# Retention takes one finished normalized input, with three gate tiles ahead of queries and keys

## The chip, the core and the metric

The kernel runs on one core of a Trainium2 chip. The metric is the device time of one execution in microseconds; three runs of the kernel before took 1112.13, 1111.17 and 1109.13 us, median 1111.17 us. The engines are named as in the profile: PE is the matrix engine (PEld its weight loads), DVE the vector engine, ACT the scalar engine, POOL GpSimd, SP the engine that issues the loads.

## The reference

Two layers; each is a SwiGLU half step, a token mixer and a second SwiGLU half step, all on a normalized and modulated input. The mixer of layer 0 is retention, that of layer 1 a short convolution. For x of 256 tokens by 1024 features the mixer's part is:

```python
h = modulate(x, norm_g[l, 1], shift[:, 1], scale[:, 1])  # x / rms(x) * g * (1 + scale) + shift
proj = h @ w_in                                          # q, k: 4 heads x 256; v: 4 x 512; g: 2048
q = rotary(q, pos)
k = rotary(k, pos) * (dk ** -0.5)
# x1 * cos - x2 * sin, x2 * cos + x1 * sin
o = ...            # decayed causal attention per head: (q k^T * decay) v, in chunks
o = rmsnorm(o, gn_g.reshape(H, dv))
y = (jax.nn.silu(g) * o.reshape(B, S, H * dv)) @ w_out
x = x + gate[:, 1, None, :] * y
```

## The kernel before

Features lie on the 128 partitions, tokens along the free dimension; x is eight blocks of 128 x 256. Every float32 operand of a large product is split in two halves, a high one and a low one (type fp32r); a product is high x high + high x low + low x high, so three matmuls for each 128 x 128 block of weights (`product`, lines 273 to 287). Where the two halves of the moving operand lie side by side and the result has room for both, the first two are one matmul of 512 columns (line 283); otherwise they are two (lines 285 and 286), and line 287 is the third.

Weights come in tiles of 2048 columns, 16 blocks of 128, in the order of the list `jobs` (lines 199 to 218); `weights()` takes the next one, keeps four loads ahead and every now and then adds a load of conditioning weights whose reduction runs on DVE (line 119). Each tile is split in two parts of 1024: the high half by ACT (line 243), the low half by DVE or, for some, POOL (line 248). Buffers hold three split tiles (six parts).

While x gets its last residual, the next stage's input is already prepared as h = x * scale, not yet divided by the rms and without the shift (`scaled`, lines 374 to 397). Each h block has 256 token columns and two more columns that hold the shift, so each matmul streams 258 columns, and a projection leaves in column 256 what the shift contributes. r = 1/rms is applied when the result is taken out of PSUM: `normalized` (lines 302 to 308) multiplies a pair of output blocks, 2 x 258, by r; the shift's part is then added as a bias. `modulated` (lines 411 to 423) starts the first tile before r is known and hands it on as `begun`.

Retention (lines 598 to 717) runs eight query/key tiles, four value heads of two weight tiles each, eight gate tiles, eight output tiles. For each query/key tile, line 610 adds std times the shift's part, `rotate` (lines 589 to 596) makes the rotation from SBUF with six operations of 256 elements, half on POOL and half on DVE, with tables that line 603 has multiplied by r. Beside each of these tiles one block of a second input, `hv` (lines 617 to 619), is made for the values: x * scale + std * shift, in halves; it stands as the weights' side in the value products (lines 632 to 634), where r is a factor of each token, applied when the values leave PSUM (line 637); `by_token` (lines 578 to 587) turns r for that by four matmuls. Scores (lines 640 to 658), values (660 to 678) and the norm of each head (680 to 687) follow in steps, one head behind the other; the gate tiles' outputs are made one tile at a time (lines 703 to 713): Silu, product with the normalized head, split in halves on ACT and POOL.

A planner orders each engine's queue from the program's order and the operands' readiness; every engine then works through its queue in that order, and an instruction that waits holds those behind it. PSUM is four buffers of two banks. One pool of 22 slots of 128 x 512 (`slot`, line 82) holds `qk`, `hv`, `v`, `sc`, `o`, `og` and, in other stages, `act` and `conv`; a slot is free when the last reader of its tile is done.

Of the kernel before, what the change touches and what calls it, by code (L numbers as in the profile page):

```python
# [9 lines left out]
F32 = mybir.dt.float32  # L10
# [4 lines left out]
P = 128  # L15
# [15 lines left out]
LATE = 5  # L31
AHEAD = 4
# [33 lines left out]
def trunk_kernel(ctx: ExitStack, tc: tile.TileContext, a: dict, out: bass.AP):  # L66
# [135 lines left out]
    for l in range(DEPTH):  # L202
        for f in range(2):
            if f == 1:
                if l % 2 == 0:
                    jobs += [(a["ret_qk"][j], 2048) for j in range(8)]
                    jobs += [(a["ret_v"][h, i], 2048) for h in range(HEADS) for i in range(2)]
                    jobs += [(a["ret_g"][j], 2048) for j in range(8)]
# [80 lines left out]
    def projections(h, by_part=False):  # L289

        ps, w = banks(), weights()
        n = h[0].shape[-1]
# [7 lines left out]
        return ps  # L300

# [103 lines left out]
    def fill(n):  # L405

        ps = banks()[:, 1, :P]
        for _ in range(n):
            nc.tensor.matmul(out=ps, lhsT=ones, rhs=cond[:, :P], start=True, stop=True)

# [167 lines left out]
    def by_token(r):  # L578

        ps = banks()  # L580
        t = tmp.tile([P, 2], F32, name="by_token")
        for tb in range(2):
            nc.tensor.matmul(
                out=ps[:, tb, :1], lhsT=r[:1, tb * P:(tb + 1) * P], rhs=ones[:1, :1], start=True, stop=True
            )
        nc.vector.tensor_copy(out=t, in_=ps[:, :, 0])
        return [t[:, tb:tb + 1] for tb in range(2)]

    def rotate(y, cos, sin, dst):
        t = tmp.tile([P, 2, S], F32, name="rot", tag="rot")  # L590
        nc.gpsimd.tensor_tensor(out=t[:, 0, :], in0=y[:, 1, :S], in1=sin, op=ALU.mult)
        nc.vector.tensor_tensor(out=t[:, 1, :], in0=y[:, 1, :S], in1=cos, op=ALU.mult)
        nc.gpsimd.tensor_tensor(out=dst[:, :S], in0=y[:, 0, :S], in1=cos, op=ALU.mult)
        nc.gpsimd.tensor_tensor(out=dst[:, :S], in0=dst[:, :S], in1=t[:, 0, :], op=ALU.subtract)
        nc.vector.tensor_tensor(out=dst[:, S:], in0=y[:, 0, :S], in1=sin, op=ALU.mult)
        nc.vector.tensor_tensor(out=dst[:, S:], in0=dst[:, S:], in1=t[:, 1, :], op=ALU.add)

    def retention(n, h, r, std, begun):
        l, s = sublayers[n]
        cos = table[:, T_COS:T_COS + S]  # L600
        sin = table[:, T_SIN:T_SIN + S]
        for t in (cos, sin):
            nc.gpsimd.tensor_tensor(out=t, in0=t, in1=r[:, :S], op=ALU.mult)
        qk = []
        hv = []
        while len(qk) < 2 * HEADS:
            ps = projections(h) if qk else begun
            y = tmp.tile([P, 2, HALF], F32, name="sum")
            for i in range(2):
                nc.vector.scalar_tensor_tensor(  # L610
                    out=y[:, i, :S], in0=std, scalar=ps[:, i, S:S + 1], in1=ps[:, i, :S], op0=ALU.mult, op1=ALU.add
                )
            t = slot(F32, "qk")
            rotate(y, cos, sin, t)
            qk.append(t)
            k = len(qk) - 1
            xs = tmp.tile([P, S], F32, name="xs", tag="av", bufs=3)
            nc.scalar.activation(out=xs, in_=x[k], func=AF.Copy, scale=scale_t[l][s][:, k:k + 1])
            hv.append(halves(l, s, k, xs, std, in_halves(slot(F32R, "hv")))[0])
        r_tok = by_token(r)  # L620
        v = [[] for _ in range(HEADS)]

        def project_values(hd):
# [11 lines left out]
            for tb in range(2):  # L635
                t = slot(F32, "v")
                nc.scalar.activation(out=t, in_=ps[:, tb, :], func=AF.Copy, scale=r_tok[tb])
                v[hd].append(t)
# [51 lines left out]
        gated = []  # L690
        steps = [lambda hd=hd: project_values(hd) for hd in range(HEADS)]
        steps += [lambda j=j: projections(h) for j in range(8)]
        for step, run in enumerate(steps):
            got = run()
# [164 lines left out]
```

## Time and profile before

| | us |
|---|---|
| median of three runs | 1111.17 |
| the profiled execution | 1109.17 |
| its span, first to last instruction | 1107.4 |
| PE busy in the span | 1073.8 |
| DVE busy | 850.2 |
| ACT busy | 575.4 |
| POOL busy | 387.7 |

The profile is of one execution, and 1.8 us of its time lie outside its span. Busy is the time in which an engine has at least one instruction running; matmuls overlap, so the busy time of PE is not its work at its peak, and the distance between the starts of two matmuls says more than the duration of one. The retention stage begins in the profile with the first matmul of 258 columns at 206.45 us and ends with its outputs at about 428 us. Wherever the text names a line, it is a line of the kernel before.

### The profile page before, as it was taken

Reading aid. Unit: us, or ns where it says so; the run is one execution under the profiler, and the core shown is the slowest. Engines: PE = TensorE matmul, PEld = TensorE weight load, DVE = VectorE, ACT = ScalarE, POOL = GpSimd, SP = SyncE. Lnnn points to the kernel's source line nnn. Section 1 sums busy time; section 2 is a strip of 40 time slices with the busy share of each in tenths; the row PEclk is TensorE's granted clock in tenths of the full one; section 3 lists DMA queues with packets and bytes.
Section 4 is the critical chain, followed back from the end, with each engine's and each line's share of the span. In section 5 each row is a group of like instructions: output and inputs, shape, how many; then the busy total and the mean of one; then the engine's idle time right before and its main releaser. Section 6 shows DMA issues by size and latency. Waiting matters only on the chain.

```text
span 1107.4 us, 19630 instructions
## 1 busy us (share of the span) xinstructions
PE 1073.8 (97%) x7790; PEld 1019.1 (92%) x7790; DVE 850.2 (77%) x1118; ACT 575.4 (52%) x918; POOL 387.7 (35%) x345
## 2 busy tenths in 40 slices
PE   8999999997899999999999999999999989999996
PEld 7999988996779989999988999998899989999985
DVE  5999777999559888887768778776798786666354
ACT  4464454732357666455455655445565475454452
POOL 0034356344024631333355232335511532223352
PEclk9999999998999999999999999999999999999998
DMA  9977789855465777786669867667886535454441
GB/s 348 354 272 277 295 283 316 308 205 190 190 228 191 265 249 278 289 312 247 244 225 321 326 251 301 253 229 252 313 300 253 175 138 207 167 191 132 157 131 39
DMA packets 44574, 268.52 MB, mean 242 GB/s; under 512 B 4801, under 2 KB 6977, under 8 KB 19906
## 3 DMA queue, kind: packets, MB, share of 16 engines
q1 hardware_dynamic: 43138, 266.56, 66.4%
q8 instruction: 61, 1.00, 0.4%
q10 hardware_dynamic: 1344, 0.71, 0.2%
q14 instruction: 31, 0.25, 0.1%
HBM read 266.20 MB, written 1.05 MB: 241 GB/s over the span
## 4 chain that ended last, share of the span: by engine, by line
PE 58%; DVE 2%; issue 0%; ACT 0%; DVEq 0%; ACTq 0%
PE ps L287 19%; PE ps L286 14%; PE ps L285 14%; PE ps L283 10%; DVE lo L248 1%; PE ps L338 0%; DVE rsum L475 0%; DVE h L392 0%; DVE raw L781 0%; DVE r L777 0%; DVE x L478 0%; ACT hi L243 0%; DVEq L854 0%; DVE x L480 0%; ACT std L350 0%
## 5 line engine op out<-in xcount | busy, mean ns | idle before, releaser
L248 DVE TENSOR_TENSOR lo<-raw,hi 128x1024 fp32r<-128x1024 f32 (+1 forms) x300 | 363.1, 1218 | 174.8 <-ACT hi L243 144.6
L285 PE MATMUL ps<-h,hi 128*128 128x258 f32 (+1 forms) x1728 | 490.2, 284 | 3.6 <-DVE sum L610 2.5
L286 PE MATMUL ps<-h,hi 128*128 128x258 f32 (+1 forms) x1728 | 489.9, 283 | 1.6 <-DVE h L392 1.5
L287 PE MATMUL ps<-h,lo 128*128 128x258 f32 (+1 forms) x1728 | 490.3, 284 | 0.0
L243 ACT CAST hi<-raw 128x1024 fp32r<-128x1024 f32 (+2 forms) x408 | 377.3, 937 | 205.8 <-PE ps L286 104.5
L285 PEld LDWEIGHTS ps<-h,hi 128*128 128x128 f32 x1728 | 329.4, 191 | 4.5 <-issue 3.2
L286 PEld LDWEIGHTS ps<-h,hi 128*128 128x128 f32 x1728 | 329.0, 190 | 2.6 <-DVE h L392 1.3
L287 PEld LDWEIGHTS ps<-h,lo 128*128 128x128 f32 x1728 | 329.0, 190 | 0.0
L248 POOL TENSOR_TENSOR lo<-raw,hi 128x384 fp32r<-128x384 f32 (+1 forms) x108 | 203.2, 1882 | 311.4 <-ACT hi L243 302.0
L283 PE MATMUL ps<-act,hi 128*128 128x512 f32 x616 | 216.0, 395 | 0.6 <-DVE rsum L475 0.6
L287 PE MATMUL ps<-act,lo 128*128 128x256 f32 x704 | 197.4, 280 | 0.0
L312 POOL TENSOR_TENSOR act<-av,act 128x256 fp32r<-128x256 f32 x88 | 84.4, 961 | 250.6 <-ACT act L311 241.5
L119 DVE CUSTOM_DVE_ANT_0 raw<-raw,ps,misc 128x1024 f32<-128x1024 f32 x124 | 154.4, 1273 | 0.0
L283 PEld LDWEIGHTS ps<-act,hi 128*128 128x128 f32 x616 | 115.4, 187 | 28.1 <-DVE rsum L475 1.7
L287 PEld LDWEIGHTS ps<-act,lo 128*128 128x128 f32 x704 | 133.1, 189 | 0.3 <-DVE lo L248 0.3
L311 ACT CAST act<-av 128x256 fp32r<-128x256 f32 x88 | 35.5, 405 | 100.8 <-DVE av L554 78.6
L305 DVE TENSOR_TENSOR sum<-ps,r 128x516 f32<-128x516 f32 (+1 forms) x108 | 73.9, 688 | 16.1 <-PE ps L287 15.8
L554 DVE SCALAR_TENSOR_TENSOR av<-sum,sg 128x256 f32<-128x256 f32 x66 | 51.8, 784 | 17.6 <-ACT sg L553 17.6
L553 ACT ACTIVATE sg<-sum 128x256 f32<-128x256 f32 x66 | 33.5, 508 | 25.7 <-DVE sum L305 25.5
L321 ACT ACTIVATE sq<-x 128x256 f32<-128x256 f32 x48 | 19.8, 416 | 49.5 <-DVE x L478 42.3
L328 POOL TENSOR_TENSOR acc<-acc,sq 128x256 f32<-128x256 f32 x32 | 27.1, 846 | 36.9 <-ACT sq L321 34.4
L283 PE MATMUL ps<-og,hi 128*128 128x512 f32 x112 | 38.9, 391 | 0.0
(126 smaller groups left out, 1079.2 us busy)
## 6 DMA issues: line engine op xcount, KB each, us to landing
raw<-in_ffn_in SPq DMA_DIRECT2D x80, 1024.0 KB, 4.9
raw<-in_ada_w SPq DMA_DIRECT2D x64, 1024.0 KB, 5.7
raw<-in_ffn_out SPq DMA_DIRECT2D x64, 704.0 KB, 5.0
raw<-in_ada_w SPq DMA_DIRECT2D x16, 512.0 KB, 6.1
raw<-in_ffn_in SPq DMA_DIRECT2D x16, 512.0 KB, 7.0
raw<-in_ret_qk SPq DMA_DIRECT2D x8, 1024.0 KB, 6.4
raw<-in_ret_v SPq DMA_DIRECT2D x8, 1024.0 KB, 4.9
raw<-in_ret_g SPq DMA_DIRECT2D x8, 1024.0 KB, 4.8
```

Source lines behind the costliest of these rows:

```text
L119: ins = nc.vector.tensor_tensor_reduce(out=w, in0=w, in1=state["cond"], scale=1.0, scalar=misc[:, C_ADAB + 72 * l + col:C_ADAB + 72 * l + ...
L243: nc.scalar.copy(out=hi, in_=raw[:, c:c + m])
L248: eng.tensor_tensor(out=lo, in0=raw, in1=hi, op=ALU.subtract)
L283: nc.tensor.matmul(out=ps, lhsT=hi, rhs=m.rearrange("p n s -> p (n s)"), start=start, stop=False)
L285: nc.tensor.matmul(out=ps, lhsT=hi, rhs=m[:, 0], start=start, stop=False)
L286: nc.tensor.matmul(out=ps, lhsT=hi, rhs=m[:, 1], start=False, stop=False)
L287: nc.tensor.matmul(out=ps[:, :n], lhsT=lo, rhs=m[:, 0], start=False, stop=stop)
L305: nc.vector.tensor_tensor(out=y[:, :, :n], in0=ps[:, :, :n], in1=r[:, :n].unsqueeze(1).to_broadcast([P, 2, n]), op=ALU.mult)
L311: hi = nc.scalar.copy(out=dst[:, 0], in_=src)
L312: lo = eng.tensor_tensor(out=dst[:, 1], in0=src, in1=dst[:, 0].bitcast(F32), op=ALU.subtract)
L553: nc.scalar.activation(out=sg, in_=y[:, 0, :S], func=AF.Silu, bias=y[:, 0, S:S + 1])
L554: nc.vector.scalar_tensor_tensor(out=av, in0=y[:, 1, :S], scalar=y[:, 1, S:S + 1], in1=sg, op0=ALU.add, op1=ALU.mult)
```

## The change

Retention no longer uses the prepared h beyond three gate tiles. A new helper, `whole`, makes its finished input, x * r * scale + shift, block by block: product with r on DVE or POOL in turn, `Identity` with scale and shift on ACT, split in halves on ACT and DVE. During this the first three gate tiles run as before, on h with its two extra columns, the first of them `begun`; their weights move to the front of the list. Queries, keys, values and the other five gate tiles use the finished input. So their results need neither r nor a bias: the rotation reads PSUM directly, two products of 2 x 256 on DVE and two operations of 256 on POOL; the values leave PSUM as a copy; `by_token`, the products of the tables by r and the bias of line 610 go. The five gate tiles use the form of 512 columns, and the second half of their result is copied by ACT and added by DVE. Silu of a gate is kept in a slot, and `apply` multiplies it with its head when that head is normalized.

```diff
@@ -29,6 +29,7 @@
 LATE = 5
+BIASED = 3
 AHEAD = 4
@@ -203,9 +204,10 @@
                 if l % 2 == 0:
+                    jobs += [(a["ret_g"][j], 2048) for j in range(BIASED)]
                     jobs += [(a["ret_qk"][j], 2048) for j in range(8)]
                     jobs += [(a["ret_v"][h, i], 2048) for h in range(HEADS) for i in range(2)]
-                    jobs += [(a["ret_g"][j], 2048) for j in range(8)]
+                    jobs += [(a["ret_g"][j], 2048) for j in range(BIASED, 8)]
                     outputs.append(len(jobs))
@@ -286,10 +288,10 @@
-    def projections(h, by_part=False):
+    def projections(h, by_part=False, side=False):
         ps, w = banks(), weights()
-        n = h[0].shape[-1]
+        n = h[0].shape[-1] * (2 if side else 1)
         if by_part:
@@ -298,6 +300,24 @@
         return ps
+
+    def projected(src):
+
+        src["used"] += 1
+        if src["used"] <= BIASED:
+            y = normalized(src.pop("begun") if src["used"] == 1 else projections(src["h"]), src["r"])
+            return y, [y[:, i, S:S1] for i in range(2)]
+        ps = projections(src["whole"], src["used"] == BIASED + 1, True)
+        y = tmp.tile([P, 2, HALF], F32, name="sum")
+        nc.scalar.copy(out=y[:, :, :S], in_=ps[:, :, S:])
+        nc.vector.tensor_tensor(out=y[:, :, :S], in0=ps[:, :, :S], in1=y[:, :, :S], op=ALU.add)
+        return y, None
+
+    def silu(y, i, bias, out):
+        if bias is None:
+            nc.scalar.activation(out=out, in_=y[:, i, :S], func=AF.Silu)
+        else:
+            nc.scalar.activation(out=out, in_=y[:, i, :S], func=AF.Silu, bias=bias[i][:, :1])
@@ -407,6 +427,22 @@
             nc.tensor.matmul(out=ps, lhsT=ones, rhs=cond[:, :P], start=True, stop=True)
+
+    def whole(n, r):
+
+        l, s = sublayers[n]
+        parts = []
+        for k in range(KB):
+            xr = tmp.tile([P, S], F32, name="xr", tag="sq", bufs=3)
+            (nc.gpsimd if k % 2 else nc.vector).tensor_tensor(out=xr, in0=x[k], in1=r[:, :S], op=ALU.mult)
+            nc.scalar.activation(
+                out=xr, in_=xr, func=AF.Identity, scale=scale_t[l][s][:, k:k + 1],
+                bias=mod[l][:, 24 * s + k:24 * s + k + 1],
+            )
+            h = in_halves(slot(F32R, "whole"))
+            split(h, xr, nc.vector)
+            parts.append(h)
+        return parts
@@ -575,49 +611,37 @@
-    def by_token(r):
-
-        ps = banks()
-        t = tmp.tile([P, 2], F32, name="by_token")
-        for tb in range(2):
-            nc.tensor.matmul(
-                out=ps[:, tb, :1], lhsT=r[:1, tb * P:(tb + 1) * P], rhs=ones[:1, :1], start=True, stop=True
+    def rotate(ps, cos, sin, dst):
+        a = tmp.tile([P, 2, S], F32, name="cosines", tag="rot")
+        b = tmp.tile([P, 2, HALF], F32, name="sines", tag="sum")[:, :, :S]
+        for t, angle in ((a, cos), (b, sin)):
+            nc.vector.tensor_tensor(
+                out=t, in0=ps[:, :, :S], in1=angle.unsqueeze(1).to_broadcast([P, 2, S]), op=ALU.mult
             )
-        nc.vector.tensor_copy(out=t, in_=ps[:, :, 0])
-        return [t[:, tb:tb + 1] for tb in range(2)]
-
-    def rotate(y, cos, sin, dst):
-        t = tmp.tile([P, 2, S], F32, name="rot", tag="rot")
-        nc.gpsimd.tensor_tensor(out=t[:, 0, :], in0=y[:, 1, :S], in1=sin, op=ALU.mult)
-        nc.vector.tensor_tensor(out=t[:, 1, :], in0=y[:, 1, :S], in1=cos, op=ALU.mult)
-        nc.gpsimd.tensor_tensor(out=dst[:, :S], in0=y[:, 0, :S], in1=cos, op=ALU.mult)
-        nc.gpsimd.tensor_tensor(out=dst[:, :S], in0=dst[:, :S], in1=t[:, 0, :], op=ALU.subtract)
-        nc.vector.tensor_tensor(out=dst[:, S:], in0=y[:, 0, :S], in1=sin, op=ALU.mult)
-        nc.vector.tensor_tensor(out=dst[:, S:], in0=dst[:, S:], in1=t[:, 1, :], op=ALU.add)
-
-    def retention(n, h, r, std, begun):
-        l, s = sublayers[n]
+        nc.gpsimd.tensor_tensor(out=dst[:, :S], in0=a[:, 0, :], in1=b[:, 1, :], op=ALU.subtract)
+        nc.gpsimd.tensor_tensor(out=dst[:, S:], in0=a[:, 1, :], in1=b[:, 0, :], op=ALU.add)
+
+    def retention(n, src):
         cos = table[:, T_COS:T_COS + S]
         sin = table[:, T_SIN:T_SIN + S]
-        for t in (cos, sin):
-            nc.gpsimd.tensor_tensor(out=t, in0=t, in1=r[:, :S], op=ALU.mult)
+        src["whole"] = whole(n, src["r"])
+        gates = []
+
+        def gate():
+            y, bias = projected(src)
+            sg = slot(F32, "gate").rearrange("p (n s) -> p n s", n=2)
+            for i in range(2):
+                silu(y, i, bias, sg[:, i, :])
+            gates.append(sg)
+
+        for _ in range(BIASED):
+            gate()
+        hv = src["whole"]
         qk = []
-        hv = []
         while len(qk) < 2 * HEADS:
-            ps = projections(h) if qk else begun
-            y = tmp.tile([P, 2, HALF], F32, name="sum")
-            for i in range(2):
-                nc.vector.scalar_tensor_tensor(
-                    out=y[:, i, :S], in0=std, scalar=ps[:, i, S:S + 1], in1=ps[:, i, :S], op0=ALU.mult, op1=ALU.add
-                )
             t = slot(F32, "qk")
-            rotate(y, cos, sin, t)
+            rotate(projections(hv, not qk), cos, sin, t)
             qk.append(t)
-            k = len(qk) - 1
-            xs = tmp.tile([P, S], F32, name="xs", tag="av", bufs=3)
-            nc.scalar.activation(out=xs, in_=x[k], func=AF.Copy, scale=scale_t[l][s][:, k:k + 1])
-            hv.append(halves(l, s, k, xs, std, in_halves(slot(F32R, "hv")))[0])
-        r_tok = by_token(r)
         v = [[] for _ in range(HEADS)]
@@ -634,7 +658,7 @@
                 t = slot(F32, "v")
-                nc.scalar.activation(out=t, in_=ps[:, tb, :], func=AF.Copy, scale=r_tok[tb])
+                nc.scalar.copy(out=t, in_=ps[:, tb, :])
                 v[hd].append(t)
@@ -688,29 +712,28 @@
         gated = []
+
+        def apply():
+            j = len(gated) // 2
+            for i in range(2):
+                ob = o[j // 2][2 * (j % 2) + i]
+                nc.vector.tensor_tensor(out=ob, in0=ob, in1=gates[j][:, i, :], op=ALU.mult)
+                t = in_halves(slot(F32R, "og"))
+                split(t, ob, nc.gpsimd)
+                gated.append(t)
+
         steps = [lambda hd=hd: project_values(hd) for hd in range(HEADS)]
-        steps += [lambda j=j: projections(h) for j in range(8)]
+        steps += [gate for _ in range(BIASED, 8)]
         for step, run in enumerate(steps):
-            got = run()
+            run()
             if step == 0:
 ...
                 raw_o[step - 1] = values(step - 1, sc[step - 1])
-            if step < HEADS:
-                continue
-            j = step - HEADS
-            y = normalized(got, r)
-            sg = tmp.tile([P, 2, S], F32, name="sgg", tag="rot")
-            for i in range(2):
-                nc.scalar.activation(out=sg[:, i, :], in_=y[:, i, :S], func=AF.Silu, bias=y[:, i, S:S + 1])
-            for i in range(2):
-                ob = o[j // 2][2 * (j % 2) + i]
-                nc.vector.tensor_tensor(out=ob, in0=ob, in1=sg[:, i, :], op=ALU.mult)
-                t = in_halves(slot(F32R, "og"))
-                split(t, ob, nc.gpsimd)
-                gated.append(t)
+            while len(gated) // 4 in o and len(gated) // 2 < len(gates):
+                apply()
         before_residuals(n)
@@ -766,7 +789,7 @@
         elif l % 2 == 0:
-            retention(n, h, r, std, begun)
+            retention(n, {"h": h, "r": r, "begun": begun, "used": 0})
         else:
```

## Rows read from the trace of the kernel before

**Rows 1.** The page, busy time, share and instructions of each engine.
```profile
PE 1073.8 (97%) x7790; PEld 1019.1 (92%) x7790; DVE 850.2 (77%) x1118; ACT 575.4 (52%) x918; POOL 387.7 (35%) x345
```
**Rows 2.** Waits of PE, 206 to 345 us: waiter, releaser, total us, times, longest.
```profile
PE ps L632 <- DVE sum L610: 5.6, 1, 5.6
PE ps L645 <- DVE sc L657: 3.4, 1, 3.4
PE ps L583 <- DVE sum L610: 2.5, 1, 2.5
PE ps L285 <- DVE sum L610: 2.5, 1, 2.5
PE ps L667 <- ACT std L350: 1.2, 1, 1.2
```
**Rows 3.** Windows: length, busy PE, PEld, DVE, ACT, POOL (instructions), clock, DMA, GB/s.
```profile
206.00:290.00 84.00, 70.05 (x479) 65.96 (x478) 80.90 (x113) 31.37 (x43) 31.48 (x30) 0.91 0.60 223
290.00:383.00 93.00, 91.81 (x597) 84.65 (x596) 67.44 (x87) 56.99 (x91) 34.78 (x33) 0.99 0.56 212
```
**Rows 4.** Windows of 8 us in which the granted clock is below 1.
```profile
238.00:246.00 8.00, 5.51 (x40) 5.33 (x40) 8.00 (x14) 2.80 (x4) 1.90 (x3) 0.91 0.62 224
246.00:254.00 8.00, 8.00 (x61) 8.00 (x60) 8.00 (x10) 1.86 (x3) 5.46 (x5) 0.87 0.54 202
262.00:270.00 8.00, 3.52 (x8) 2.81 (x9) 8.00 (x11) 2.70 (x4) 4.23 (x5) 0.50 0.56 219
270.00:278.00 8.00, 8.00 (x32) 6.30 (x31) 7.40 (x13) 1.88 (x3) 3.43 (x4) 0.88 0.37 132
286.00:294.00 8.00, 6.37 (x23) 5.30 (x24) 3.16 (x10) 0.00 (x0) 0.00 (x0) 0.79 0.72 292
```
**Rows 5.** Groups by line and shape, 206 to 290 us: busy us, mean ns, idle before.
```profile
L596 DVE TENSOR_TENSOR qk<-qk,rot 128x256 f32<-128x256 f32 x8 | 9.9, 1234 | 0.0
L592 DVE TENSOR_TENSOR rot<-sum,table 128x256 f32<-128x256 f32 x8 | 7.6, 952 | 0.0
L402 DVE SCALAR_TENSOR_TENSOR xs<-std,mod,xs 128x256 f32<-128x256 f32 x8 | 7.6, 951 | 0.0
L610 DVE SCALAR_TENSOR_TENSOR sum<-std,ps 128x256 f32<-128x256 f32 x16 | 6.9, 472 | 0.0
L595 DVE TENSOR_TENSOR qk<-sum,table 128x256 f32<-128x256 f32 x8 | 6.4, 797 | 0.5 <-POOL table L603 0.5
L594 POOL TENSOR_TENSOR qk<-qk,rot 128x256 f32<-128x256 f32 x8 | 6.4, 796 | 0.6
L312 DVE TENSOR_TENSOR hv<-xs,hv 128x256 fp32r<-128x256 f32 x8 | 3.3, 413 | 0.1
L618 ACT ACTIVATE xs<-x,sc 128x256 f32<-128x256 f32 x5 | 2.6, 510 | 9.5 <-DVE hv L312 9.5
```
**Rows 6.** Line 305 in the whole span: ns shortest/median/longest, first and last start, forms.
```profile
L305 DVE TENSOR_TENSOR sum<-ps,r x108: 674/689/697, 60.6 to 1034.6; 128x516 f32<-128x516 f32 x86, 128x512 f32<-128x512 f32 x22
```
**Rows 7.** Timeline, start us, us, then the instruction: single rows near 206 and 215 to 223.
```profile
206.45 0.28 PE L285 MATMUL ps<-h,hi 128*128 128x258 f32 x1
...
215.51 1.74 DVE L356 RECIPROCAL r<-std 128x256 f32<-128x256 f32 x1
...
222.04 2.56 POOL L248 TENSOR_TENSOR lo<-raw,hi 128x1024 fp32r<-128x1024 f32 x1
...
222.28 2.60 DVE L596 TENSOR_TENSOR qk<-qk,rot 128x256 f32<-128x256 f32 x1
```
**Rows 8.** Timeline of PE: six triples of 258 columns, eight pairs of 512 and 256.
```profile
364.53 0.28 PE L285 MATMUL ps<-h,hi 128*128 128x258 f32 x1
...
366.70 0.28 PE L285 MATMUL ps<-h,hi 128*128 128x258 f32 x1
...
398.94 0.39 PE L283 MATMUL ps<-og,hi 128*128 128x512 f32 x1
...
401.71 0.39 PE L283 MATMUL ps<-og,hi 128*128 128x512 f32 x1
```

## The prediction

> **What bounds the kernel now.** I read the page's busy times first: TensorE (PE) is busy 1073.8 of 1107.4 us [rows 1], so the span is its work plus what it waits, and a change pays where it takes away one of the two. The waits of PE in the retention stage come next. Five of them add up to 15.2 us [rows 2]: 2.5 us inside the query/key tiles, 2.5 us ahead of the by-token transposition (line 583), 5.6 us ahead of the first value product (line 632), 3.4 us in the scores (line 645) and 1.2 us behind the square root of a head. That is 15.2 of the 33.6 us that PE idles in the whole span. Four of the five end with an instruction of VectorE (DVE), lines 610 and 657.
>
> The third view, the windows, says why: from 206 to 290 us DVE is busy 80.90 of 84.00 us while PE is busy 70.05 [rows 3]. Here DVE sets the pace. The same windows show a second price. Around each long wait the granted clock falls, to 0.50 in the worst window [rows 4]: PE runs at 1.2 GHz instead of 2.4 while it works again. Busy time there by the missing share of the clock: 0.09 x 5.51 + 0.13 x 8 + 0.50 x 3.52 + 0.12 x 8 + 0.21 x 6.37 = 5.6 us. Waits and clock together are 20.8 us that this stage loses to DVE and to the order of its work.
>
> **DVE: what goes and what comes.** Of the 80.90 us, the groups by line give what the change removes [rows 5]: the bias added to two halves of eight tiles (line 610, 6.9 us), three rotation operations a tile (lines 592, 595, 596: 7.6 + 6.4 + 9.9 us) and the multiply-add by std for the value input (line 402, 7.6 us): 38.4 us. The low half of the value input (line 312, 3.3 us) stays, under another name.
>
> What comes: two products a query/key tile, 512 elements wide, straight from PSUM, 16 in all. Line 305 is that form (PSUM times a row broadcast over two halves): 108 of them lie between 674 and 697 ns [rows 6]. I take 0.68 us: 10.9 us. Four products by r on DVE, between 0.41 (line 312, same shape from SBUF) and 0.95 us (line 592) [rows 5]: I take the upper end, 3.8 us, since POOL makes the other four beside them. The evictions of three gate tiles, 0.69 us each, 2.1 us, are moved here from behind.
>
> A row shows why line 596 is dear: at 222.28 it takes 2.60 us where the same shape at line 312 averages 0.41; a POOL low half (line 248) of 2.56 us began just before it [rows 7]. The 108 operations from PSUM show no such stretch [rows 6]. So the rotation products leave the operations that POOL can stretch, while the four products by r and the weights' low halves stay among them. The Trainium skill (SBUF — State Buffer, section "SBUF: two separate sides") says that the port pair which DVE and GpSimd share is an exclusive lock, and lists a DVE operation with two SBUF inputs among its users. That speaks against the new products, half on each engine: by that rule a pair costs the sum of both, about 1.2 us (0.41 and POOL's 0.80), against 0.95 by the row, 1 us more in all.
>
> Does DVE then fit? Without the removed work it had 42.5 us left, of which 3.3 is line 312, so about 39 us for roughly 11 tiles of weights (low halves, conditioning reductions) and some singles: 3.6 us a tile. The new stage has three more tiles in it: 14 x 3.6 + 3.3 + 10.9 + 3.8 + 2.1 = 70 us. PE's own work there is 70.05 - 5.6 = 64.5 us plus three gate tiles. A product of 3 x 258 columns takes (366.70 - 364.53) / 6 = 0.362 us [rows 8], a tile has 16 of them, 5.8 us, so 64.5 + 17.4 = 82 us. DVE is at 85%: no longer the pace, but without much room.
>
> **PE's own work.** The five late gate tiles change from 3 x 258 columns to 512 + 256: eight such pairs at line 283 take 401.71 - 398.94 = 2.77 us, 0.346 each [rows 8]. 80 products x 0.016 = 1.2 us gained, at most; at least nothing. The eight query/key tiles go from 258 to 256 columns: by the columns 128 x 0.362 x 2/258 = 0.4 us; at least nothing, and at most, if they came to the rate of the pair, 2.0. I take 1.4 us for both, bounds 0 to 3.2. The four tiny matmuls of line 583 go too; their price is the 2.5 us wait already counted.
>
> **What moves.** Three gate tiles come ahead of the query/key tiles: for each its 1 MB load, two high halves on ACT, two low halves on DVE or POOL, 48 matmuls, an eviction and two Silu. The loads of all three kinds have one size, so SP's queue, which they are moved past, only changes the order of equal loads: nothing. On POOL two products by r on the table go; the four new products come ahead of the low half at 222.04 us. On ACT the eight passes over x stay eight (now Identity), the eight high halves stay, and five copies of 512 elements from PSUM come, each below two of line 618's 0.51 us; ACT is busy 31.37 of 84 us [rows 3], so this lies beside PE. Without that cover it would be at most 5 us.
>
> The gates are applied when their head is normalized, some of it now during the value products, where the tail of the stage had all of it. No work is added by that, but the last gate's eviction, Silu, product and split still follow the last gate tile, under the first output products that want those parts last.
>
> **The new wait.** The first query/key tile now needs the finished input. r is ready at 215.51 + 1.74 = 217.25 us [rows 7]. One block takes 0.95 (product) + 0.51 (ACT, line 618) + about 0.41 (its high half, as the DVE operation of that shape) + 0.41 (low half, line 312) [rows 5] = 2.3 us; three buffers let them overlap, so one follows every 0.9 or so, ACT's two passes. First block at about 220, last at about 227. PE began the stage at 206.45 [rows 7] and works three gate tiles first, 17.4 us and a little for the sum of squares: it asks for the first block at about 224.2 and, block by block, two products of 0.36 apart, for the last at 229.3. Two microseconds of slack, then. Queued behind the waiting Identity on ACT are the next weights' high halves, behind the products on DVE their low halves and the reductions; those are wanted a tile later, at 230. DVE has about 14 us of work queued between 217 and 230 (whole input 7, two evictions 1.4, low halves and reductions 6): it may be late by a little. I put 1.5 us of PE wait here, bounds 0 and 4.
>
> **The sum.** Removed: 15.2 + 5.6 + 1.4 = 22.2 us. Kept: the 1.2 us behind the square root (that chain is not touched), 1.0 of the 3.4 us in the scores (PSUM is still evicted behind weights' work on DVE, which arrives less late). New: 1.5 at the whole input, 1.0 for the tail of the gates, which now has five tiles of cover and not eight. Net 22.2 - 4.7 = 17.5. The profiled execution took 1109.17 us, so 1091.7; it lies 2.0 us under the median of the three runs, so the median to expect is 1111.17 - 17.5 = 1093.7, rounded to **1093**.
>
> **Rivals.** (a) DVE stays late. POOL has 16 additions of 0.80 us [rows 5] and four products; if all 16 us of it stretches DVE's low halves and products, DVE needs 86 us against PE's 82, and with the 6 us by which it is late at the start some 6 us of waits and 4 us of low clock come back: 1093 + 10 = 1103. Against it: DVE's 3.6 us a tile already holds such stretches. (b) The whole input is late by its full bound, 4 us and a little clock: 1097. (c) The change doesn't do what it says: the work that leaves the first half returns in the second, where five tiles cover the gates instead of eight and DVE was already full; PE waits there what it saved, 1109. The 290 to 383 row speaks against it, DVE 67.44 of 93.00 [rows 3]. (d) The other side: the pool of 22 slots. The finished input holds 8 of them to the last gate tile (the value input was free after the values), three early gates hold 3, the queries and keys 8, values 2, scores one at a time: 21 or 22 at the scores, and by my count of the code 21 to 23 wanted in the value steps. It decides from the point where a value or output tile must wait for a head to be gated: the chain of that head (copies, squares, square root, reciprocal, products, split) is about 9 us, and three heads in that position give 27 us: 1093 + 27 = 1120. For it: the count touches 22. Against it: each tile that asks last is made from tiles that its own matmuls release.
>
> **How the numbers follow.** Forecast (1088 to 1096): 0.60. (a) 0.17. (b) 0.08. (c) 0.07. (d) 0.08. Faster by over 0.3% (about what a measurement of this kernel tells from no change) holds forecast, (a) and (b): 0.85; within 0.3% (c): 0.07; slower (d): 0.08. The range takes in (a) and (b) and, below, the bounds of the unknown terms (streaming +1.8, whole input +1.5, the rest of the kept waits +3): 1086 to 1106.
>
> **What would show it.** Right: in the changed profile DVE below 90% from 206 to 290 us, no PE wait over 2 us before the scores, the granted clock at 1.00 through the query/key tiles, and no line of DVE that ends a wait of line 632. PE asks for the first query/key tile near 224. Wrong: a wait of that tile's first matmuls on the input's low half (b); DVE still at 8.00 of 8.00 with the clock below 1.00 (a); PE waiting on ACT or POOL in the value steps or the outputs (d); idle time of PE in the five late gates or the first outputs as long as what the first half saved (c).

## The result and the profile after

The changed kernel takes **1094.97 us** (median of four runs, 1094.53 to 1095.29) against 1111.24 for the kernel before beside it. The ratio is 0.9857, 95% interval 0.9845 to 0.9869: 16.3 us faster, where 17.5 was worked out and 1093 forecast. The profiled execution took 1094.71 us with a span of 1092.9, so 14.5 us less than the profiled one of before (1109.17 us; the other runs of before took 1109.13 to 1112.13).

The page after gives PE's busy time and its share, then the other engines, to be laid beside [rows 1]. All lines of code in the rows of this part are lines of the changed kernel.

```profile
PE 1067.8 (98%) x7706; PEld 1008.9 (92%) x7706; DVE 830.8 (76%) x1089; ACT 578.0 (53%) x923; POOL 391.0 (36%) x339
```

PE idles 25.1 us of its span, where it idled 33.6. DVE lost 19.4 us of work. The waits of PE from 200 to 420 us (waiter, releaser, total us, times, longest) answer to [rows 2]; the last line belongs to the start of the next stage and was there before too, with 0.6 us.

```profile
PE ps L691 <- ACT std L370: 2.2, 2, 1.2
PE ps L285 <- DVE sum L313: 1.9, 1, 1.9
PE ps L287 <- ACT whole L331: 1.1, 1, 1.1
PE ps L358 <- POOL acc L348: 1.0, 1, 1.0
PE ps L288 <- DVE whole L332: 0.9, 1, 0.9
PE ps L288 <- DVE h L412: 0.6, 1, 0.6
```

The first five lines are 7.1 us where five others were 15.2, and none of the old ones but that of std is left. The windows (length, busy PE, PEld, DVE, ACT, POOL, clock, DMA, GB/s) answer to [rows 3, 4]:

```profile
206.00:290.00 84.00, 82.00 (x620) 79.06 (x620) 71.75 (x96) 42.14 (x61) 36.36 (x29) 1.00 0.74 277
290.00:383.00 93.00, 87.95 (x461) 75.16 (x460) 67.00 (x85) 59.45 (x103) 43.10 (x42) 1.00 0.53 195
...
262.00:270.00 8.00, 8.00 (x69) 8.00 (x68) 7.84 (x11) 2.74 (x4) 3.26 (x3) 1.00 0.81 306
286.00:294.00 8.00, 8.00 (x44) 6.92 (x43) 2.62 (x9) 0.69 (x2) 0.00 (x0) 1.00 0.55 213
```

From 206 to 290 us PE is busy 82.00 us instead of 70.05 and DVE 71.75 instead of 80.90. The stretch from 262 to 270 us, where the clock stood at 0.50, now runs full at 1.00, and so does every window of 8 us up to 294.

**Where the 14.5 us are.** Three marks bound the stage. In the timeline of PE (start us, us, instruction) of the changed kernel, the third of the five late gates, the first output tile and the first matmul of the next stage begin here:

```profile
351.01 0.58 PE L285 MATMUL ps<-whole,hi 128*128 128x512 f32 x1
...
367.85 0.39 PE L285 MATMUL ps<-og,hi 128*128 128x512 f32 x1
...
412.42 0.28 PE L287 MATMUL ps<-h,hi 128*128 128x258 f32 x1
```

And the same in the timeline of the kernel before, with its own lines; its first mark is the third gate tile of eight:

```profile
348.43 0.47 PE L285 MATMUL ps<-h,hi 128*128 128x258 f32 x1
...
383.34 0.39 PE L283 MATMUL ps<-og,hi 128*128 128x512 f32 x1
...
427.91 0.28 PE L285 MATMUL ps<-h,hi 128*128 128x258 f32 x1
```

From the stage's first matmul, at 206.45 before [rows 7] and 206.43 after, to the next stage it is 221.5 us and 206.0: 15.5 less. Waits give 15.2 - 7.1 = 8.1 of it and the clock 5.6. A gate tile took (383.34 - 348.43) / 6 = 5.82 us and takes (367.85 - 351.01) / 3 = 5.61, which makes 1.0 over five. The query/key tiles give about 0.2 by two columns fewer, and the rest of 0.6 fits the four matmuls of `by_token` in the kernel before:

```profile
260.33 0.57 PE L583 MATMUL ps<-ones,r 1*128 1x1 f32 x4 [2.53 <-DVE sum L610]
```

The pieces are good to about half a microsecond. The 5.6 us of the clock are worked out from windows of 8 us, and [rows 4] leave out the one from 254 to 262, which stands at 0.98 (0.1 us more); by windows of 2 us the same working gives 6.0. Behind the stage 1.0 us is lost again (680.5 us to the end of the span instead of 679.5); that is within what single runs differ by.

### The profile page after: what moved, and what is told of

Same layout as the page of the kernel before. It is cut to its first block, busy times and chain, and to the rows that moved or that the text cites. A ratio compares the mean times of both kernels' runs of the same rounds, so it can differ in the third digit from the quotient of the medians.

```text
span 1092.9 us, 19439 instructions
## 1 busy us (share of the span) xinstructions
PE 1067.8 (98%) x7706; PEld 1008.9 (92%) x7706; DVE 830.8 (76%) x1089; ACT 578.0 (53%) x923; POOL 391.0 (36%) x339
## 4 chain that ended last, share of the span: by engine, by line
PE 59%; DVE 2%; issue 0%; ACT 0%; DVEq 0%; ACTq 0%
PE ps L289 20%; PE ps L288 14%; PE ps L287 14%; PE ps L285 11%; DVE lo L250 1%; PE ps L358 0%; DVE rsum L511 0%; DVE h L412 0%; DVE raw L804 0%; DVE r L800 0%; DVE x L514 0%; ACT hi L245 0%; DVEq L877 0%; DVE x L516 0%; ACT std L370 0%
## 5 line engine op out<-in xcount | busy, mean ns | idle before, releaser
L288 PE MATMUL ps<-h,hi 128*128 128x258 f32 (+1 forms) x1520 | 430.4, 283 | 1.7 <-DVE h L412 1.5
L287 PE MATMUL ps<-h,hi 128*128 128x258 f32 (+1 forms) x1520 | 430.5, 283 | 1.1 <-DVE sum L325 1.1
L289 PE MATMUL ps<-h,lo 128*128 128x258 f32 (+1 forms) x1520 | 430.5, 283 | 0.0
L250 POOL TENSOR_TENSOR lo<-raw,hi 128x384 fp32r<-128x384 f32 (+1 forms) x108 | 201.5, 1867 | 290.4 <-ACT hi L245 290.0
L288 PEld LDWEIGHTS ps<-h,hi 128*128 128x128 f32 x1520 | 288.7, 190 | 2.6 <-DVE h L412 1.3
L287 PEld LDWEIGHTS ps<-h,hi 128*128 128x128 f32 x1520 | 289.0, 190 | 1.8 <-ACT sg L586 0.7
L289 PEld LDWEIGHTS ps<-h,lo 128*128 128x128 f32 x1520 | 288.7, 190 | 0.0
L325 DVE TENSOR_TENSOR sum<-ps,r 128x516 f32<-128x516 f32 (+1 forms) x103 | 70.7, 690 | 16.1 <-PE ps L289 15.8
L289 PE MATMUL ps<-whole,lo 128*128 128x256 f32 x208 | 58.5, 281 | 0.0
L589 ACT ACTIVATE sg<-sum 128x256 f32<-128x256 f32 x66 | 33.6, 509 | 26.3 <-DVE sum L325 25.9
```

The lines of the kernel that those rows point to most:

```text
L250: eng.tensor_tensor(out=lo, in0=raw, in1=hi, op=ALU.subtract)
L287: nc.tensor.matmul(out=ps, lhsT=hi, rhs=m[:, 0], start=start, stop=False)
L288: nc.tensor.matmul(out=ps, lhsT=hi, rhs=m[:, 1], start=False, stop=False)
L289: nc.tensor.matmul(out=ps[:, :n], lhsT=lo, rhs=m[:, 0], start=False, stop=stop)
L325: nc.vector.tensor_tensor(out=y[:, :, :n], in0=ps[:, :, :n], in1=r[:, :n].unsqueeze(1).to_broadcast([P, 2, n]), op=ALU.mult)
L589: nc.scalar.activation(out=sg, in_=y[:, 0, :S], func=AF.Silu, bias=y[:, 0, S:S + 1])
```

## The experiments

Unless said otherwise, waits and windows are read as above. Each ratio is against the kernel before, run on the same chip. The runs stand on several chips, so runs of different chips are to be compared by their ratios (0.001 is 1.1 us). The yardstick is the changed kernel run again:

> The changed kernel as it is, on the chip and beside the runs of the next three, as their yardstick. All theories: 1093 to 1096 us, PE waits of 7 us in the stage, clock 1.00 in its windows.

Measured: 1095.41 us, ratio 0.9865 (0.985 to 0.988), with the same waits.

### Was DVE's load the cause?

**The changed kernel with the old rotation**, its six operations preceded by two copies out of PSUM:

```diff
-        for t, angle in ((a, cos), (b, sin)):
-            nc.vector.tensor_tensor(
...
+        for i in range(2):
+            nc.vector.tensor_copy(out=y[:, i, :S], in_=ps[:, i, :S])
+        t = tmp.tile([P, 2, S], F32, name="rot", tag="rot")
+        nc.gpsimd.tensor_tensor(out=t[:, 0, :], in0=y[:, 1, :S], in1=sin, op=ALU.mult)
...
```

> The changed kernel with one part undone: the rotation again takes its input out of PSUM with two copies of 256 on DVE and makes six operations of 256, half on DVE, half on POOL. Everything else is the changed kernel. Theory (DVE's load sets the pace of the query/key tiles): DVE gets back about 6.9 + 23.9 - 10.9 = 20 us in this stretch, is at 95% or more of 206 to 290 us, and PE waits of 5 us or more with a clock below 1.00 come back: 1101 to 1107 us. Rival (the order of the work, the finished input and the end of the by-token step are what counts): below 1098 us, PE waits in the stage under 9 us.

Measured: 1103.41 us, ratio 0.9943 (0.9922 to 0.9965), so 8 to 9 us of the gain are gone. The largest wait of PE, in the first line, and two windows of this kernel:

```profile
PE ps L671 <- ACT v L663: 7.1, 1, 7.1
...
206.00:290.00 84.00, 77.02 (x586) 74.26 (x585) 82.65 (x110) 38.08 (x56) 42.76 (x36) 1.00 0.65 244
286.00:294.00 8.00, 1.81 (x4) 1.52 (x5) 7.33 (x12) 2.11 (x4) 0.89 (x1) 0.71 0.76 298
```

DVE is back at 82.65 of 84 us (20 us were expected back, and the window has no room for more than 84), and one wait of 7.1 us comes back with a clock of 0.71 around it. It stands at the scores (line 671) and is put down to ACT's eviction of values (line 663). ACT's timeline shows what held the eviction up:

```profile
289.94 0.19 ACT L331 CAST h<-mod 128x2 fp32r<-128x2 f32 x1 [7.71 <-DVE mod L120]
...
290.98 1.06 ACT L663 COPY v<-ps 128x512 f32<-128x512 f32 x2
```

A small cast in front of it waited 7.71 us for a reduction of DVE, so DVE owes this wait too. The debt no longer ends in the query/key tiles; it is carried forward and paid at the scores. The other waits of this kernel are those of the changed one. The change without its new rotation still gains 6.4 us (1109.79 to 1103.41).

**The kernel before without DVE's part of the rotation.** This is the other direction, with nothing else of the change:

```diff
-        nc.vector.tensor_tensor(out=t[:, 1, :], in0=y[:, 1, :S], in1=cos, op=ALU.mult)
-        nc.vector.tensor_tensor(out=dst[:, S:], in0=y[:, 0, :S], in1=sin, op=ALU.mult)
-        nc.vector.tensor_tensor(out=dst[:, S:], in0=dst[:, S:], in1=t[:, 1, :], op=ALU.add)
+        nc.scalar.copy(out=dst[:, S:], in_=y[:, 0, :S])
```

> The kernel before with DVE's three rotation operations left out; the second half of each rotated tile is a plain copy on ACT, POOL's three operations stay. So part of the rotation is not computed. Theory (DVE's load): DVE loses 23.9 us of 80.9, PE's waits fall from 15.2 us to about 5 and the granted clock stays at 1.00: 1094 to 1100 us without any other part of the change. Rival (order and by-token step): 1106 to 1111 us.

Measured: 1096.21 us, ratio 0.9877 (0.9859 to 0.9896), nearly the whole gain of the change. Its waits and its window:

```profile
PE ps L643 <- DVE sc L655: 3.8, 1, 3.8
PE ps L665 <- ACT std L350: 1.2, 1, 1.2
PE ps L630 <- DVE sum L608: 1.1, 1, 1.1
...
206.00:290.00 84.00, 79.12 (x532) 73.87 (x531) 72.45 (x92) 38.82 (x59) 39.51 (x31) 0.98 0.64 239
```

The waits inside the query/key tiles and ahead of the transposition are gone, that of the values is 1.1 us instead of 5.6, and the clock of the stretch is 0.98 instead of 0.91. Not all came as expected: 3.8 us at the scores stay, and the clock falls around them (0.79 from 270 to 278 us), where 1.00 was expected throughout. This kernel leaves out a part of the rotation; what it shows is what DVE's work costs. DVE at 72.45 of 84 us is enough for most of the gain, with the old input. The 13.6 us here and the 6.4 us above come to more than the change's 16.3, so the two parts are not separate shares of it.

### Or was it the place of the transposition?

`by_token` stood between the last query/key tile and the values, so its wait might have been its own doing. **The kernel before with `by_token` at the stage's start:**

```diff
+        r_tok = by_token(r)
         qk = []
...
-        r_tok = by_token(r)
         v = [[] for _ in range(HEADS)]
```

> The kernel before with one thing moved: the by-token transposition stands at the start of retention, so that its four matmuls and its PSUM buffer no longer lie between the last query/key tile and the values. Rival (this step's buffer holds up the values): the 2.5 us wait at the transposition and the 5.6 us wait behind it go, with 2 to 3 us of low clock: 1101 to 1104 us. Theory (DVE is late and only shows there): the values start earlier but wait for DVE's low halves of the value input instead; 1108 to 1112 us, no measurable gain.

Measured: 1106.28 us, ratio 0.997 (0.996 to 0.9979), between the two expectations. Its largest waits:

```profile
PE ps L634 <- DVE hv L312: 5.3, 2, 3.9
PE ps L583 <- DVE r L356: 4.4, 1, 4.4
PE ps L645 <- DVE sc L657: 2.2, 1, 2.2
```

This edit brought a wait of its own, 4.4 us for r, which is not ready so early, and the order of the debts changed with it. So it could not tell the two apart. **The same, with `by_token` behind the rotation of the fourth tile**, where r has long been there (`len(qk)` is 3 at that point; the expectation counts it as the third):

```diff
             rotate(y, cos, sin, t)
+            if len(qk) == 3:
+                r_tok = by_token(r)
...
-        r_tok = by_token(r)
```

> The kernel before with the by-token transposition after the third query/key tile, where r has long been ready and a PSUM buffer is free. In the earlier run at the very start PE waited 4.4 us for r there, which hid what the step costs where it stood. Rival (its place and its PSUM buffer cost about 8 us of the 15.2): 1102 us or less, PE waits in the stage under 9 us. Theory (DVE is late and every freed wait comes back at the next thing that DVE owes): 1105 to 1109 us, with a wait of about 5 us for the low half of the value input.

Measured: 1107.13 us, ratio 0.9979 (0.997 to 0.9989). Its waits:

```profile
PE ps L285 <- DVE sum L610: 6.0, 2, 5.0
PE ps L633 <- ACT hv L311: 5.4, 1, 5.4
PE ps L646 <- DVE sc L658: 1.5, 1, 1.5
```

With the std line of 1.2 us and one of 0.6 they sum to 14.7 us, against 15.2; DVE is busy 80.56 of 84. The longest waits are again for what DVE owes: the bias (line 610), and the high half of the value input (line 311), which ACT could make only when DVE had made its input (line 402). The waits only change their place. Moving the transposition is worth 3.5 us in the one run and 1.9 in the other, and not the gain; what its four matmuls themselves cost is the 0.6 us above.

### What are the waits that remain?

**The whole input.** The blocks' products and passes, in the changed kernel (ns shortest/median/longest, first and last start, forms):

```profile
L438 ACT ACTIVATE xr<-xr,mod,sc x8: 586/602/605, 218.7 to 227.9; 128x256 f32<-128x256 f32 x8
...
L437 POOL TENSOR_TENSOR xr<-x,r x4: 798/860/1601, 217.0 to 226.5; 128x256 f32<-128x256 f32 x4
L437 DVE TENSOR_TENSOR xr<-x,r x4: 411/413/964, 217.9 to 226.4; 128x256 f32<-128x256 f32 x4
```

The last products start at 226.5 us: eight in 9.5 us, one every 1.4 us and not 0.9. DVE's timeline shows what stands between them:

```profile
222.45 0.41 DVE L437 TENSOR_TENSOR xr<-x,r 128x256 f32<-128x256 f32 x1
222.79 1.27 DVE L120 CUSTOM_DVE_ANT_0 raw<-raw,ps,misc 128x1024 f32<-128x1024 f32 x1
...
223.99 1.27 DVE L120 CUSTOM_DVE_ANT_0 raw<-raw,ps,misc 128x1024 f32<-128x1024 f32 x1
...
225.19 1.26 DVE L332 TENSOR_TENSOR whole<-xr,whole 128x256 fp32r<-128x256 f32 x2
```

A reduction in two parts, 222.79 to 225.26, stands ahead of two low halves. On POOL the fourth product waited 0.70 us for a low half to give its buffer back. I had two theories for it. **The order:** the whole input given a higher priority in the planner.

```diff
-        src["whole"] = whole(n, src["r"])
+        with tc.high_priority(PRIO):
+            src["whole"] = whole(n, src["r"])
```

> The changed kernel with the finished input at high priority for the planner, ahead of the conditioning reductions and the weights' low halves that lie between its blocks now. Theory (the two waits of the first query/key tile, 1.1 and 0.9 us, come from those in DVE's and POOL's queues): both waits go, the last block is ready before 227 us, 1093 us, unless the weights' low halves are late instead. Rival (the chain of passes itself is too slow): the waits stay within 0.5 us of 2.0; 1095 us.

Measured: 1095.64 us, ratio 0.9872 (0.9851 to 0.9893), with the same two waits of 1.1 and 0.9 us. The order of these instructions did not change, so this run tells nothing of either theory. **The buffers:** xr takes turns in two sets of three instead of one.

```diff
-            xr = tmp.tile([P, S], F32, name="xr", tag="sq", bufs=3)
+            xr = tmp.tile([P, S], F32, name="xr", tag="av" if k % 2 else "sq", bufs=3)
```

> The changed kernel with six buffers instead of three for the blocks of the finished input on their way (two names of three buffers in turn). Theory (three buffers make a block wait for the low half of the third before it, so the planner lets a reduction of 2.4 us and a POOL low half of 2.4 us in between): the eight blocks follow each other without these, PE's two waits of 1.1 and 0.9 us at the first query/key tile go, 1093 us. Rival (the two passes of ACT set the time of the eight blocks, 8 x 1.0 us): at least 1 us of the waits stays, 1094.5 to 1095 us.

Measured: 1091.62 us, ratio 0.9846 (0.9832 to 0.9861). DVE's timeline and the window of this kernel:

```profile
223.98 0.41 DVE L437 TENSOR_TENSOR xr<-x,r 128x256 f32<-128x256 f32 x1
224.32 0.75 DVE L332 TENSOR_TENSOR whole<-xr,whole 128x256 fp32r<-128x256 f32 x2
224.99 1.27 DVE L120 CUSTOM_DVE_ANT_0 raw<-raw,ps,misc 128x1024 f32<-128x1024 f32 x1
...
206.00:290.00 84.00, 84.00 (x630) 81.00 (x629) 71.77 (x96) 41.57 (x61) 36.49 (x29) 1.00 0.73 279
```

The last product comes at 223.98 us, the reduction behind it, both input waits are gone, and PE is busy 84.00 of 84.00 us. By the ratios it is 2.1 us faster than the yardstick, and 2.0 us of waits are gone. The same work on DVE, 71.77 us, with other buffers: the buffers had set the pace of the input, one product every 1.4 us with three and every 1.0 us with six.

**Two early gates instead of three**, which gives the input 5.8 us less cover:

```diff
-BIASED = 3
+BIASED = 2
```

> The changed kernel with two gate tiles ahead of the queries and keys instead of three. Theory (the early tiles are the cover of the finished input, whose last block is ready near 231 us): PE asks for the first block at 218.4, 5.8 us earlier, and waits for all of it, so its waits there grow from 2.0 to about 8 us, and the clock falls once: 1099 to 1103 us. Rival (the cover is ample and the wait comes from elsewhere): within 1.5 us of the yardstick.

Measured: 1097.44 us, ratio 0.9884 (0.987 to 0.9899), 2.0 us over the changed kernel on the same chip (1095.41). The direction was as expected, the size not. Its waits:

```profile
PE ps L285 <- DVE sum L313: 2.3, 1, 2.3
PE ps L287 <- ACT whole L331: 2.3, 2, 2.1
PE ps L669 <- DVE sc L681: 1.6, 1, 1.6
PE ps L288 <- DVE whole L332: 1.3, 2, 1.0
```

The input's waits are 3.6 us instead of 2.0, not 8: the last block was made by 228.6 us, where it was 231.4 with three gates (1.3 of these 2.8 us because the stage began earlier). The clock did fall once, as expected, but later, around the wait of 2.3 us in the late gates: the granted clock was 0.84 from 342 to 350 us. What the input takes is not a fixed time behind r; it depends on the work that is queued between its blocks. The third early gate is worth 2 us.

**The gates' tail.** DVE's timeline in the changed kernel, ahead of the wait at line 285, and PE's row behind it:

```profile
340.64 1.27 DVE L120 CUSTOM_DVE_ANT_0 raw<-raw,ps,misc 128x1024 f32<-128x1024 f32 x1
...
341.84 1.27 DVE L120 CUSTOM_DVE_ANT_0 raw<-raw,ps,misc 128x1024 f32<-128x1024 f32 x1
...
343.04 0.68 DVE L313 TENSOR_TENSOR sum<-ps,sum 128x512 f32<-128x512 f32 x1
...
343.78 0.50 PE L285 MATMUL ps<-whole,hi 128*128 128x512 f32 x1 [1.91 <-DVE sum L313]
```

The addition that empties the PSUM of a late gate stands behind a reduction of 2.4 us, and PE waits 1.91 us for the buffer. So the next kernel **makes late gates as 3 x 256 and lets Silu read PSUM**, with neither copy nor addition:

```diff
-        ps = projections(src["whole"], src["used"] == BIASED + 1, True)
-        y = tmp.tile([P, 2, HALF], F32, name="sum")
-        nc.scalar.copy(out=y[:, :, :S], in_=ps[:, :, S:])
-        nc.vector.tensor_tensor(out=y[:, :, :S], in0=ps[:, :, :S], in1=y[:, :, :S], op=ALU.add)
-        return y, None
+        return projections(src["whole"], src["used"] == BIASED + 1), None
```

> The changed kernel with one part undone and one cut short: the five late gate tiles use three matmuls of 256 again instead of 512 and 256, and Silu reads PSUM itself, so ACT's copy of 512 and DVE's addition of 512 go. Theory (the wait of 1.9 us in the late gates is that addition, queued behind DVE's reductions): that wait goes; PE's five tiles take 80 x about 0.010 = 0.8 us more by the triples and pairs in the trace; 1093.5 to 1094.5 us. Rival (the 512-wide form is worth its full bound, and PE waits elsewhere instead): 1096 us or more.

Measured: 1093.40 us, ratio 0.9863 (0.9843 to 0.9883). The waits of 1.9 and 1.0 us are gone and one of 0.9 for Silu is new, 2.0 us less in all. By the ratio the time moved by 0.2 us, far less than its interval, so a gain of this edit by itself is not shown. The gates give back what the form of 512 columns had gained them, 1.0 at most. And in the trace of this kernel (1096.19 us) the two waits of the input, 1.1 and 0.9 us as before, brought the clock down:

```profile
230.00:238.00 8.00, 7.83 (x53) 7.83 (x53) 6.63 (x11) 4.59 (x7) 0.10 (x1) 0.79 0.74 258
```

In the traces of the changed kernel this window stands at 1.00. So two waits of about 1 us can cost the clock or not.

**Both edits together:**

> The two edits of the six buffers and of the gates read from PSUM together. If both waits are what they seem, the gains add: about 1092 us, PE waits in the stage near 3 us (square root 2.2, one sum of squares). If the second only moves a wait into the first output products or the heads' norms: 1094 us or more.

Measured: 1090.18 us, ratio 0.9834 (0.9818 to 0.9851), 1.4 us less than with the six buffers alone on the same chip; the two intervals overlap. The waits left are 2.2 for std and 0.9 for a gate. **And with these, the next head's value products ahead of the norm of the head before,** since it is value products (line 691) that wait for std:

```diff
-            if 0 <= step - 2 < HEADS:
-                o[step - 2] = normalize(step - 2, *raw_o[step - 2])
             if 0 <= step - 1 < HEADS:
                 raw_o[step - 1] = values(step - 1, sc[step - 1])
+            if 0 <= step - 2 < HEADS:
+                o[step - 2] = normalize(step - 2, *raw_o[step - 2])
```

> The run with both edits (six buffers, gates from PSUM) and, besides, the values of a head ahead of the norm of the head before it in the program. Theory (the 2.2 us of waits behind the square root are a PSUM buffer that the sum of squares holds while ACT loads a table and takes the root): they go, 1088 to 1089 us. Rival (the buffer is short in either order): they stay at about 2 us or a head's norm is late at the gates, 1090 to 1092 us.

Measured: **1088.26 us**, ratio 0.9801 (0.9786 to 0.9815), the best of all: 7.1 us under the changed kernel on the same chip. All its waits of PE from 200 to 425 us:

```profile
PE ps L354 <- ACT gate L314: 1.5, 1, 1.5
PE ps L354 <- POOL acc L344: 0.3, 1, 0.3
```

1.8 us are left of 7.1, so 5.3 us of waits are gone. How much of the time belongs to the edits can be read from the marks of the stage: from its first matmul to the next stage it is 201.5 us in this trace and 206.1 in the yardstick's, 4.6 less. The two traces differ by 7.8 us in all; the rest lies ahead of the stage (1.4 us) and behind it (1.8 us), in code that the three edits leave as it is, and no run shows that it is theirs.

### Slots

**The changed kernel with 24 slots** instead of 22:

```diff
-    slot_p = ctx.enter_context(tc.tile_pool(name="slot", bufs=22))
+    slot_p = ctx.enter_context(tc.tile_pool(name="slot", bufs=24))
```

> The changed kernel with 24 slots instead of 22. Rival of the prediction (the pool of slots holds up a value, a gate or a gated head): the waits of 1.9 and 1.0 us in the late gates change or go, over 1 us faster than the yardstick. Theory (each tile that asks last is made from tiles that its own matmuls release): within 1 us of the yardstick, the same five waits.

Measured: 1096.62 us, ratio 0.9875 (0.9858 to 0.9892), with the same five waits. That is 1.2 us over the yardstick, where 1 us at most was expected, and the intervals overlap. 0.8 us of it lie in the output tiles, which run without a wait (45.3 us where the yardstick's trace has 44.6); the cause is open. The pool of 22 holds nothing up.

## Why the prediction was right, and where it was off

**What bounds it: right.** PE's waits fell when DVE lost work in the kernel before (15.2 to 6.1 us) and came back, at another place, when it got work back in the changed one (7.1 to 14.3). The place of the transposition as the main cause is excluded by the run with it in the middle: 14.7 us of waits remain.

**The clock: right.** 5.6 us were claimed and every window stands at 1.00 now. It is the second half of a long wait's price: where 7.1 us came back, so did a clock of 0.71.

**DVE's account: right to 2 us.** 70 us were forecast for 206 to 290, 71.75 measured; for PE 82 and 82.00. PE asked for the first query/key block at 224.24 us, for which 224.2 was worked out.

**Four terms of what stays or comes were mis-sized.** (The sum itself ends in 1093.7, which rounds to 1094; 1093 was put down.) Together they are 7.1 us where 4.7 stood in the sum. These 2.4 and the 1.0 us behind the stage, less 0.4 by which PE's own work shrank more than I had taken (1.0 + 0.2 + 0.6 against 1.4), are the 3.0 us from 1091.7 to 1094.71. It was luck that the 1.0 us put down for the scores, which did not come, covers half of what the tail was short of.

| term | in the sum | measured |
|---|---|---|
| square root of a head | 1.2 | 2.2, two heads instead of one |
| scores | 1.0 | 0 |
| whole input | 1.5 | 2.0 |
| gates' tail | 1.0 | 2.9 (1.9 at line 313, 1.0 at line 358) |

For the *whole input* the price was near, but the working was not: three buffers were taken to let the blocks overlap at one per 0.9 us, and the buffers made it 1.4. The first blocks were in time and the last were not, at 229.81 and 231.10 us. One pass of `Identity` with scale and bias took 0.60 us, where 0.51 of the old `Copy` stood in its place. For the *gates' tail* I counted the cover in tiles, and the wait came from a queue: an addition behind a reduction. Its second wait, 1.0 us ahead of the third late gate, is for the sum of squares of the last head (line 358); it went with the same edit. DVE was busy 67.00 of 93 us in that stretch, which does not help the one instruction that stands behind two long ones. The *square root* was priced as untouched, and for the first head it was. The second head's wait, which was not there before, is again a queue behind DVE, as ACT's timeline of the changed kernel shows:

```profile
330.13 0.19 ACT L331 CAST h<-mod 128x2 fp32r<-128x2 f32 x1 [1.43 <-DVE mod L120]
...
331.17 0.47 ACT L370 ACTIVATE std<-ps,eps 128x256 f32<-128x256 f32 x1
```

The root stands behind a weight's high half and a small cast that waited 1.43 us for a reduction of DVE.

**PE's own work:** the gates gave 0.21 us a tile, where 0.016 x 16 = 0.26 had been read from [rows 8]; the four tiny matmuls were wrongly left out of it, as if their wait were their whole price.

**The rivals.** (a) DVE stays late: no, but the run with the old rotation is that rival made, and it gave 1103.41 where 1103 was priced. (b) The input late by 4 us: half of that came, with no loss of clock. (c) The gain returning in the second half: the tail's 2.9 us, 1.9 more than I had put there, are of that kind, so the mechanism is there, far below its price of 16. (d) The slots: they show neither as a wait of the changed kernel nor as a gain from two more.

**The shared port.** The first product on POOL took 1.60 us beside a low half and a product of DVE, against 0.80 at its shortest (line 437), and that product of DVE took 964 ns against 411. So the trace agrees with the rule that the one engine shuts the other out (the Trainium skill, SBUF — State Buffer, section "SBUF: two separate sides"). It does not agree with the price that the prediction worked out from it. With six buffers, three products of each engine met in a row:

```profile
217.68 2.74 DVE L437 TENSOR_TENSOR xr<-x,r 128x256 f32<-128x256 f32 x3
...
216.76 3.38 POOL L437 TENSOR_TENSOR xr<-x,r 128x256 f32<-128x256 f32 x3 [8.23 <-DVE r L376]
```

Three pairs took 2.74 us on DVE, about 0.9 each: the 0.95 read from the rows was right, and the sum of 1.2 was not.

## What to carry to other kernels

Read which engine owes the work that ends a run of waits, not which wait is longest: moving the instruction that waits only moves the wait, while taking work off the owing engine removed most of the waits and of the low clock around them together. That engine may stand behind another one: three times here a wait for ACT was in truth one for DVE, which ACT's own queue was waiting for. When a chain is moved into cover, count its buffers before its busy times; here they set its pace, and they decided what the planner put between its steps. Every wait that is removed lets PE arrive sooner at the next debt, so price the kept waits anew: after this change three small edits, each aimed at waits of 1 to 2 us, shortened the stage by another 4.6 us. And compare the stage, not only the whole time, when the gain is of the size by which runs differ.

## What was not expected of the hardware

A product of two SBUF operands, 128 x 256, took about twice its time on both engines where DVE and POOL met (0.96 and 1.60 us instead of 0.41 and 0.80), and yet three pairs in a row cost 0.9 us each and not the sum of both. `Identity` with a scale and a bias for each partition took 0.60 us, 0.09 more than `Copy` with a scale of the same shape [rows 5]. And PE's busy time alone hid a quarter of the loss: 5.6 of the 20.8 us stood in the granted clock while PE counted as busy.
